# A two-layer decoder trunk on one core: how the first product's token blocks are evacuated, where the first RMSNorm's squares and token scale stand, and the last piece of the output

## The chip, the core and the metric

The kernel runs on one core of one Trainium2 chip. The metric is the device time of one execution in microseconds. The core's engines are TensorE (PE in the profile, its weight loads PEld), VectorE (DVE), ScalarE (ACT), GpSimd (POOL) and SyncE (SP, which here only issues transfers). An engine works its own queue in order; semaphores hold an instruction until what it needs is done.

## What is computed

A decoder of two layers over 256 tokens of width 2048 in float32: a layer of dilated window attention and a layer of latent attention, each with a SwiGLU block, and a last RMSNorm. The change works at the very start and at the very end. The start is this, cut from the reference:

```python
def rms_norm(x, g):
    y = x32 * lax.rsqrt(jnp.mean(x32 * x32, axis=-1, keepdims=True) + NORM_EPS)
    return (y * g.astype(jnp.float32)).astype(x.dtype)
...
xn = rms_norm(h, attn_norm_g[layer])
qkv = (xn @ w_qkv).reshape(b, s, N_A_GROUPS, 3, A_HEADS, A_HEAD_DIM)
...
return rms_norm(h, final_norm_g)
```

The token scale (the rsqrt) is one number per token, so the kernel multiplies x by the gain first, starts the products at once, and applies the scale to the results.

## The kernel before

Every matrix product runs in a split form: each operand is a rounded part (`hi`, or columns 0 to 255 of a block of `xT`) and a residue (`lo`, or columns 256 to 511), and three matmuls per block and token half (hi by hi, hi by lo, lo by hi) add up in PSUM. ScalarE makes the rounded parts by a copy, VectorE the residues by subtracting.

`first_product` is the first of the products for the values of four heads (a quad), with three products (g = 0, 1, 2) of 16 blocks each (k = 0 to 15, 128 columns of x each). It runs before any transposed x exists, so it makes it on the way, in eight steps q of two blocks. `turn(q)` lets TensorE transpose two blocks of both token halves into one PSUM bank (L673). `tokens(q, kk)` takes block 2q + kk out of that bank: `put_split` writes the rounded part by ScalarE (L421) and the residue by VectorE (L422), both times the gain. `weights(q, ...)` casts the weights of the step on ScalarE (L689) and makes their residue on VectorE (L690). `products(k)` issues six matmuls (L699). After the turn of step q come the products of block 2q - 1 and 2q; after the last turn blocks 13, 14 and 15. The order on ScalarE, VectorE and TensorE in this part is that of the code (`manual_schedule`); elsewhere a scheduler may reorder.

Weights come in units through `WeightStream`: three buffers of raw weights, each refilled by SP when the residue that last read it is done; units 0 and 1 serve step 0 and 1, unit 2 steps 2 and 3, unit 3 steps 4 and 5, unit 4 steps 6 and 7. Units 5 on are the second product's, four units to a product; `product` makes hi and lo of a unit two units ahead (L152, L153) and runs `x_stationary` (L522 to L524).

`norms(i)` squares and sums one of five column pieces of x: pieces 0 and 1 on VectorE (L431), 2 to 4 on ScalarE (L434), two instructions each. `token_stats` sums the pieces (L463, L457), takes the power -0.5 on GpSimd (L458) and splits the scale into a power of two and a remainder (L471, L473). Both are spread over all partitions by a matmul (`across`: L481, L484, L485) into `R2` and `R`. `to_v` evacuates a product to v with the scale as factor (L814); until then its accumulator is held, and there are two accumulators. `by_row` (L492) scales `xT` by `R2` in place in the third product. `Later` holds closures that are called so many ticks (units) on. L315 turns the other gain vectors.

At the end, `end1` finishes the last 512 columns of each token half: add, square, power on GpSimd (L1171), and scale the whole row in five pieces, stored in four (L1182).

Of the kernel before, what the change touches and what calls it, by code (L numbers as in the profile page):

```python
# [10 lines left out]
F32 = mybir.dt.float32  # L11
# [3 lines left out]
ALU = mybir.AluOpType  # L15
# [23 lines left out]
LAG_S, LAG_V = 2, 3  # L39
WARM = 8  # L40

# [206 lines left out]
def kernel(ctx, tc, consts, x, attn_norm_g, ffn_norm_g, a_w_qkv, a_w_o, kv_norm_g,  # L248
# [21 lines left out]
    def big_tile(shape, dtype, name):  # L270
        return big.tile(shape, dtype, tag="big", name=name)
# [389 lines left out]
    ssq_x = small.tile([P, NT, len(X_CHUNKS)], F32, name="ssq_x", tag="ssq_x", bufs=1)  # L661
    xT = big_tile([P, KD, 2 * S], F32R, "xT_a")
    def first_product():

# [4 lines left out]
        def turn(q):  # L669
            banks[q] = ps = bank()  # L670
            for kk in range(2):
                for t in range(NT):
                    nc.tensor.transpose(out=ps[:, kk * S + t * P:kk * S + (t + 1) * P],  # L673
                                        in_=xt[:, t, (2 * q + kk) * P:(2 * q + kk + 1) * P], identity=ident)

        def tokens(q, kk):
            k = 2 * q + kk
            put_split(xT[:, k, 0:S], xT[:, k, S:2 * S], banks[q][:, kk * S:(kk + 1) * S], g_attn0[:, k:k + 1])

# [21 lines left out]

        def norms(i):
            c0, w = X_CHUNKS[i]
            for t in range(NT):
                squares(xt[:, t, c0:c0 + w], ssq_x[:, t, i:i + 1], on_vector=i < 2)

        with tc.manual_schedule(engines=ORDERED | {mybir.EngineType.PE}):
            turn_attn()
            turn(0)
            weights(0, (0,), nc.vector.tensor_copy)  # L710
            tokens(0, 0)
            tokens(0, 1)
            weights(0, (1,))
            ws.load(4)
            products(0)
            for q in range(1, KD // 2):
                turn(q)
                for kk in range(2):
                    if q == 1:
                        weights(q, (kk,))  # L720
                    elif kk == 0:
                        weights(q, (0, 1))
                    tokens(q, kk)
                if q in (1, 3, 5):
                    later.tick()
                    ws.load(5 + q // 2)
                if q > 2:
                    norms(q - 3)
                products(2 * q - 1)
# [13 lines left out]
    def token_stats():  # L743

        rstd = token_scale(ssq_x, "rstd")
        r2_a, rem_a = parted(rstd)
        later.put(1, lambda: row_a.update(R2=across(r2_a, "R2", ap)))
        later.put(2, lambda: row_a.update(R=across(rem_a, "R")))
        for name, src, by in (("sc", rem_a, P ** -0.5), ("nsc", rem_a, -(P ** -0.5))):
            stats[name] = small.tile([P, NT], F32, name=name, tag=name, bufs=1)  # L750
            nc.vector.tensor_scalar(out=stats[name], in0=src, scalar1=by, scalar2=None, op0=ALU.mult)
        return rstd, rem_a

# [50 lines left out]
    for quad in range(HEADS // 4):  # L804
        vs = [ap.tile([P, NT, 512], F32, tag=f"v{g}", name=f"v{g}", bufs=1) for g in range(NG)]
        seven = SEVEN_V[quad]
        if quad == 0:
            acc0 = first_product()
            rstd, rem_a = token_stats()
        rv = rem_a if seven else rstd  # L810

        def to_v(v, src, rv=rv):
            for t in range(NT):
                nc.scalar.activation(out=v[:, t, :], in_=src[:, t, :], func=AF.Copy, scale=rv[:, t:t + 1])  # L814
# [343 lines left out]
    def end1(acc, t):  # L1158
# [12 lines left out]
        nc.gpsimd.tensor_tensor(out=r, in0=v, in1=mhalf[:, :1], op=ALU.pow)  # L1171
        nc.vector.tensor_tensor(out=h, in0=h, in1=fin["g"][:, 3 * 512:], op=ALU.mult)
        for a, b, on, queue in ((0, 512, 0, nc.sync), (512, 1024, 1, nc.scalar), (1024, 1536, 0, nc.sync),
                                (1536, 1792, 1, None), (1792, 2048, 0, nc.scalar)):
            piece = stream[0][:, t, a:b]
            if on:
                nc.scalar.activation(out=piece, in_=piece, func=AF.Copy, scale=r)
            else:
                nc.vector.tensor_scalar(out=piece, in0=piece, scalar1=r, scalar2=None, op0=ALU.mult)
            if queue:  # L1180
                a = min(a, 1536)
                queue.dma_start(out=ov[:, t, a:b], in_=stream[0][:, t, a:b])  # L1182

# [31 lines left out]
```

## Time and profile before

| quantity | value |
|---|---|
| median of 3 runs | 2652.59 us (2652.28 to 2652.73) |
| profiled execution | 2653.16 us, its span from first to last instruction 2651.4 us |
| TensorE clock granted | 0.999 |
| PE busy in the first 36.2 us from 4.5 us on | 30.14 of 31.70 us |
| ScalarE and VectorE busy there | 19.30 and 19.24 us |
| ScalarE's evacuations L421 waiting for VectorE's residue L422 | 8.3 us in 8 waits |
| VectorE's weight residues L690 waiting for the cast L689 | 6.2 us in 6 waits |
| DMA share from 8 to 24 us | 1.03 to 1.06 (full) |

Times in the trace are counted from the span's start. Idle time of an engine counts only where TensorE waits for it in the end, since TensorE's busy share of the whole span is 99%.

### The profile page before, as it was taken

What the parts mean: (1) busy time and instruction counts of PE and PEld (TensorE: products, weight loads), DVE (VectorE), ACT (ScalarE), POOL (GpSimd) and SP (SyncE); (2) the same over time, 40 slices, a digit from 0 to 9 for tenths busy, and PEclk for the clock granted to TensorE, in tenths of its full rate; (3) what the DMA queues carried; (4) which work ended last, traced back from release to release, by engine and by line L of the source; (5) the groups of instructions that cost most, each with busy time, mean ns of one, the idle gap of its engine ahead of it and who ended that gap; (6) DMA issues with size and microseconds to landing.
All of it is one profiled execution on the core that took longest, in us unless ns stands there. A gap on an engine that the chain in (4) does not pass through costs nothing.

```text
span 2651.4 us, 33136 instructions
## 1 busy us (share of the span) xinstructions
PE 2636.6 (99%) x12852; PEld 2211.9 (83%) x12852; DVE 2123.7 (80%) x2513; ACT 1324.5 (50%) x1406; POOL 106.9 (4%) x120
## 2 busy tenths in 40 slices
PE   9999999999999999999999999999999999999998
PEld 7888888888888888888888888888888888888887
DVE  5776777777677789987888887688789888898886
ACT  5444444444444455554554455565555545554554
POOL 0000000000000000001001100000000001001000
PEclk9999999999999999999999999999999999999999
DMA  7544655555555557678768867544466787768875
GB/s 252 191 161 163 203 173 172 178 184 164 174 178 170 196 175 222 206 222 255 218 214 231 245 200 231 167 155 135 154 209 208 219 238 229 221 205 248 237 225 164
DMA packets 324381, 529.39 MB, mean 200 GB/s; under 512 B 17960, under 2 KB 121088, under 8 KB 323840
## 3 DMA queue, kind: packets, MB, share of 16 engines
q1 hardware_dynamic: 305200, 492.33, 56.1%
q0 software_dynamic: 18112, 33.56, 8.2%
q8 instruction: 100, 1.64, 0.3%
q10 hardware_dynamic: 912, 1.39, 0.2%
q14 instruction: 57, 0.47, 0.1%
HBM read 514.63 MB, written 2.10 MB: 195 GB/s over the span
## 4 chain that ended last, share of the span: by engine, by line
PE 96%; DVE 1%; ACT 1%; DMA 1%; issue 1%; SPq 0%; POOL 0%; POOLq 0%; DVEq 0%; ACTq 0%
PE acc L609 17%; PE acc L610 17%; PE acc L611 17%; PE acc L503 15%; PE acc L506 8%; PE bank L610 4%; PE bank L609 4%; PE bank L611 4%; PE acc L523 3%; PE acc L524 3%; PE acc L522 3%; PE bank L779 1%; PE bank L443 1%; PE bank L794 1%; PE bank L573 1%
## 5 line engine op out<-in xcount | busy, mean ns | idle before, releaser
L152 ACT CAST hi<-raw 128x2048 fp32r<-128x2048 f32 (+3 forms) x612 | 874.7, 1454 | 755.8 <-PE acc L503 281.1
L153 DVE TENSOR_TENSOR lo<-raw,hi 128x2048 fp32r<-128x2048 f32 (+3 forms) x612 | 1046.6, 1721 | 254.8 <-ACT hi L152 235.8
L609 PE MATMUL acc<-hi,xT_f 128*128 128x512 f32 x996 | 390.0, 392 | 0.0
L610 PE MATMUL acc<-lo,xT_f 128*128 128x512 f32 x996 | 388.1, 390 | 0.0
L611 PE MATMUL acc<-hi,xT_f 128*128 128x512 f32 x996 | 388.1, 390 | 0.0
L503 PE MATMUL acc<-xT_a,hi 128*128 128x512 f32 x1536 | 379.0, 395 | 0.0
L503 PEld LDWEIGHTS acc<-xT_a,hi 128*128 128x128 f32 x1536 | 281.6, 188 | 53.8
L152 ACT CAST th<-sums 128x1536 fp32r<-128x1536 f32 x104 | 154.4, 1485 | 198.8 <-DVE sums L177 125.9
L609 PEld LDWEIGHTS acc<-hi,xT_f 128*128 128x128 f32 x996 | 187.0, 188 | 39.5 <-ACT gate L959 0.8
L611 PEld LDWEIGHTS acc<-hi,xT_f 128*128 128x128 f32 x996 | 187.0, 188 | 39.4
L610 PEld LDWEIGHTS acc<-lo,xT_f 128*128 128x128 f32 x996 | 187.1, 188 | 38.8
L153 DVE TENSOR_TENSOR tl<-sums,th 128x1536 fp32r<-128x1536 f32 x104 | 182.4, 1754 | 35.3 <-ACT th L152 35.3
L506 PEld LDWEIGHTS acc<-xT_a,lo 128*128 128x128 f32 x1536 | 196.9, 191 | 7.6
L506 PE MATMUL acc<-xT_a,lo 128*128 128x256 f32 x1536 | 199.2, 283 | 0.0
L609 PE MATMUL acc<-hi,hT 128*128 128x512 f32 x412 | 161.0, 391 | 0.0
L610 PE MATMUL acc<-lo,hT 128*128 128x512 f32 x412 | 160.5, 389 | 0.0
L611 PE MATMUL acc<-hi,hT 128*128 128x512 f32 x412 | 160.5, 389 | 0.0
L177 DVE TENSOR_TENSOR sums<-raw,sums 128x1024 f32<-128x1024 f32 x104 | 127.4, 1225 | 3.5
L176 DVE TENSOR_TENSOR sums<-raw 128x512 f32<-128x512 f32 x104 | 71.5, 687 | 58.7 <-DMA raw<-in_ffn_w_down_dram 22.2
L610 PEld LDWEIGHTS acc<-lo,hT 128*128 128x128 f32 x412 | 77.4, 188 | 16.2
L611 PEld LDWEIGHTS acc<-hi,hT 128*128 128x128 f32 x412 | 77.3, 188 | 16.3
L609 PEld LDWEIGHTS acc<-hi,hT 128*128 128x128 f32 x412 | 77.4, 188 | 16.1
(357 smaller groups left out, 4090.0 us busy)
## 6 DMA issues: line engine op xcount, KB each, us to landing
raw<-in_ffn_w_gu_dram SPq DMA_DIRECT2D x292, 512.0 KB, 4.8
raw<-in_a_w_qkv_dram SPq DMA_DIRECT2D x118, 1024.0 KB, 5.0
raw<-in_ffn_w_down_dram SPq DMA_DIRECT2D x124, 512.0 KB, 5.3
raw<-in_ffn_w_gu_dram SPq DMA_DIRECT2D x120, 256.0 KB, 3.9
raw<-in_a_w_qkv_dram SPq DMA_DIRECT2D x51, 512.0 KB, 4.8
raw<-in_a_w_o_dram SPq DMA_DIRECT2D x32, 512.0 KB, 4.6
raw<-in_b_w_o_dram SPq DMA_DIRECT2D x32, 512.0 KB, 4.7
raw<-in_ffn_w_gu_dram POOLq DMA_DIRECT2D x60, 256.0 KB, 4.6
```

The lines of the kernel that those rows point to most:

```text
L152: cast = lambda: nc.scalar.copy(out=hi, in_=src)
L153: rest = lambda: nc.vector.tensor_tensor(out=lo, in0=src, in1=hi.bitcast(F32), op=ALU.subtract)
L176: tt(out=w[:, 1], in0=v[:, 0], in1=v[:, 2], op=ALU.subtract)
L177: tt(out=w[:, 0::2], in0=v[:, 1::2], in1=w[:, 1].unsqueeze(1).broadcast_to([P, 2, 512]), op=ALU.subtract)
L503: mm(out=acc[:, i, :], lhsT=sl(hi, kk), rhs=xT[:, k0 + kk, :], start=first and kk == 0, stop=False)
L506: mm(out=acc[:, i, 0:S], lhsT=sl(lo, kk), rhs=xT[:, k0 + kk, 0:S], start=False, stop=last and kk == nk - 1)
L522: mm(out=acc[:, t, :ncol], lhsT=xh, rhs=rhs(hi, kk), start=st, stop=False)
L523: mm(out=acc[:, t, :ncol], lhsT=xh, rhs=rhs(lo, kk), start=False, stop=False)
L524: mm(out=acc[:, t, :ncol], lhsT=xl, rhs=rhs(hi, kk), start=False, stop=sp)
L609: mm(out=out, lhsT=xh, rhs=wh, start=st, stop=False)
L610: mm(out=out, lhsT=xh, rhs=wl, start=False, stop=False)
L611: mm(out=out, lhsT=xl, rhs=wh, start=False, stop=sp)
```

## The change

Five things are changed. In `first_product` both blocks of a pair are evacuated by ScalarE, one after the other, and VectorE's two residues follow (`tokens`, `tokens_lo`). The squares of pieces 2 to 4 leave the first product and come one, two and three ticks into the second. `token_stats`, the two spreads and the evacuation of the first product to v come after them; the second product's order on ScalarE and VectorE is now that of the code as well. Seven matmuls on ones instead of eight open the kernel. At the end the multiplication by the final gain is no instruction of its own but part of scaling the last piece, which VectorE now does whole.

```diff
-WARM = 8
+WARM = 7
...
-        def tokens(q, kk):
+        def tokens(q, lo=(0, 1)):
+            for kk in range(2):
+                k = 2 * q + kk
+                nc.scalar.activation(out=xT[:, k, 0:S], in_=banks[q][:, kk * S:(kk + 1) * S], func=AF.Copy,
+                                     scale=g_attn0[:, k:k + 1])
+            for kk in lo:
+                tokens_lo(q, kk)
+
+        def tokens_lo(q, kk):
             k = 2 * q + kk
-            put_split(xT[:, k, 0:S], xT[:, k, S:2 * S], banks[q][:, kk * S:(kk + 1) * S], g_attn0[:, k:k + 1])
+            nc.vector.scalar_tensor_tensor(out=xT[:, k, S:2 * S], in0=banks[q][:, kk * S:(kk + 1) * S],
+                                           scalar=g_attn0[:, k:k + 1], in1=xT[:, k, 0:S].bitcast(F32),
+                                           op0=ALU.mult, op1=ALU.subtract)
...
             turn(0)
+            tokens(0, ())
             weights(0, (0,), nc.vector.tensor_copy)
-            tokens(0, 0)
-            tokens(0, 1)
+            tokens_lo(0, 0)
             weights(0, (1,))
+            tokens_lo(0, 1)
...
-                for kk in range(2):
-                    if q == 1:
-                        weights(q, (kk,))
-                    elif kk == 0:
-                        weights(q, (0, 1))
-                    tokens(q, kk)
+                if q == 1:
+                    weights(q, (0,))
+                    tokens(q, (0,))
+                    weights(q, (1,))
+                    tokens_lo(q, 1)
+                else:
+                    weights(q, (0, 1))
+                    tokens(q)
...
-                if q > 2:
+                if q in (3, 4):
                     norms(q - 3)
...
-        later.put(1, lambda: row_a.update(R2=across(r2_a, "R2", ap)))
-        later.put(2, lambda: row_a.update(R=across(rem_a, "R")))
+        later.put(2, lambda: row_a.update(R2=across(r2_a, "R2", ap)))
+        later.put(3, lambda: row_a.update(R=across(stats["rem"], "R")))
...
             acc0 = first_product()
-            rstd, rem_a = token_stats()
+            for i in range(2, len(X_CHUNKS)):
+                later.put(i - 1, lambda i=i: norms(i))
+            later.put(3, token_stats)
+            later.put(3, lambda vs=vs, acc0=acc0, to_v=to_v: to_v(vs[0], acc0))
         for g in (2,) if seven else range(NG):
+            if quad == 0 and g == 0:
+                continue
...
-            to_v(vs[g], acc0 if quad == g == 0 else product(x_stationary, xT, KD))
+            with tc.manual_schedule(engines=ORDERED) if quad == 0 and g == 1 else nullcontext():
+                acc = product(x_stationary, xT, KD)
+            to_v(vs[g], acc)
...
-        nc.vector.tensor_tensor(out=h, in0=h, in1=fin["g"][:, 3 * 512:], op=ALU.mult)
-        for a, b, on, queue in ((0, 512, 0, nc.sync), (512, 1024, 1, nc.scalar), (1024, 1536, 0, nc.sync),
-                                (1536, 1792, 1, None), (1792, 2048, 0, nc.scalar)):
...
+        for i in range(4):
+            piece = chunk(t, i)
+            if i == 3:
+                nc.vector.scalar_tensor_tensor(out=piece, in0=piece, scalar=r, in1=fin["g"][:, 3 * 512:],
+                                               op0=ALU.mult, op1=ALU.mult)
+            elif i == 1:
                 nc.scalar.activation(out=piece, in_=piece, func=AF.Copy, scale=r)
             else:
                 nc.vector.tensor_scalar(out=piece, in0=piece, scalar1=r, scalar2=None, op0=ALU.mult)
-            if queue:
...
+            (nc.sync, nc.scalar)[i % 2].dma_start(out=ov[:, t, i * 512:(i + 1) * 512], in_=piece)
```

What stands on the queues before and after. In the names, `raw` is a weight buffer as loaded, `hi` and `lo` its two parts, `bank` a pair's transposed blocks, `junk` the squares' unused output; the numbers tell buffers of one name apart. ScalarE in steps 5 and 6 of the first product, before:

```order
L689 CAST hi_244<-raw_148 128x1024
L421 ACTIVATE xT_a_118<-bank_268,g_attn_97 128x256 [waits PE_49]
L421 ACTIVATE xT_a_118<-bank_268,g_attn_97 128x256 [waits DVE_49]
L434 ACTIVATE junk_287,ssq_x_117<-xt_99 128x512 [waits DMAHW7_49]
L434 ACTIVATE junk_289,ssq_x_117<-xt_99 128x512 [waits DMAHW2_49]
L689 CAST hi_308<-raw_171 128x1024 [waits DMAHW5_49,Activation_49]
L421 ACTIVATE xT_a_118<-bank_303,g_attn_97 128x256 [waits PE_49]
L421 ACTIVATE xT_a_118<-bank_303,g_attn_97 128x256 [waits DVE_49]
```

and after:

```order
L704 CAST hi_243<-raw_147 128x1024
L684 ACTIVATE xT_a_117<-bank_267,g_attn_96 128x256 [waits PE_49]
L684 ACTIVATE xT_a_117<-bank_267,g_attn_96 128x256
L704 CAST hi_303<-raw_170 128x1024 [waits DMAHW5_49,DVE_49]
L684 ACTIVATE xT_a_117<-bank_298,g_attn_96 128x256 [waits PE_49]
L684 ACTIVATE xT_a_117<-bank_298,g_attn_96 128x256
```

The second evacuation of a pair no longer waits for VectorE, and the squares between it and the next cast are gone. VectorE at the end of the first product, before:

```order
L690 TENSOR_TENSOR lo_309<-raw_171,hi_308 128x1024 [waits Activation_49]
L422 SCALAR_TENSOR_TENSOR xT_a_118<-bank_332,g_attn_97,xT_a_118 128x256 [waits Activation_49] x2
L463 TENSOR_REDUCE ssum_372<-ssq_x_117 128x2 [waits DVE_49,Activation_49]
L457 TENSOR_SCALAR rsq_v_375<-ssum_372 128x2 [waits DVE_49]
L471 TENSOR_SCALAR r2_378<-rstd_374 128x2 [waits Pool_49]
L473 TENSOR_SCALAR rem_379<-rstd_374 128x2
L481 TENSOR_SCALAR R2_433<-ident_93,r2_378 128x128 [waits DVE_49]
L751 TENSOR_SCALAR sc_382<-rem_379 128x2 [waits DVE_49]
L751 TENSOR_SCALAR nsc_384<-rem_379 128x2
L481 TENSOR_SCALAR R2_433<-ident_93,r2_378 128x128
L153 TENSOR_TENSOR lo_354<-raw_221,hi_353 128x1024 [waits DMAHW6_49,Activation_49]
```

and after:

```order
L705 TENSOR_TENSOR lo_304<-raw_170,hi_303 128x1024 [waits Activation_49]
L691 SCALAR_TENSOR_TENSOR xT_a_117<-bank_323,g_attn_96,xT_a_117 128x256 [waits PE_49,Activation_49]
L691 SCALAR_TENSOR_TENSOR xT_a_117<-bank_323,g_attn_96,xT_a_117 128x256
L153 TENSOR_TENSOR lo_341<-raw_220,hi_340 128x1024 [waits DMAHW6_49,Activation_49]
L153 TENSOR_TENSOR lo_341<-raw_220,hi_340 128x1024 [waits Activation_49]
```

The second product's first weight residue follows the token residues directly. The second residue of a pair has no wait of its own any more, so the first one's wait covers both evacuations. The same scale instructions now stand after the residue of unit 9, the third product's first. On TensorE the seam between the products was:

```order
L699 MATMUL acc_127<-hi_308,xT_a_118 128x512
L522 MATMUL acc_388<-hi_353,xT_a_118 128x512 [waits Activation_49]
L484 MATMUL bank_436<-R2_433,ones_82 128x256 [waits DVE_49,PE_49]
L315 MATMUL bank_471<-ident_93,g_row_280 128x56 [waits DMAHW2_49,DMAHW1_49,DMAHW3_49,DMAHW0_49,PE_49]
L523 MATMUL acc_388<-lo_354,xT_a_118 128x512 [waits DVE_49]
```

and is:

```order
L714 MATMUL acc_126<-hi_303,xT_a_117 128x512
L522 MATMUL acc_361<-hi_340,xT_a_117 128x512 [waits Activation_49]
L523 MATMUL acc_361<-lo_341,xT_a_117 128x512 [waits DVE_49]
L524 MATMUL acc_361<-hi_340,xT_a_117 128x512
L522 MATMUL acc_361<-hi_340,xT_a_117 128x512
```

The spread of R2 (L484) and L315 left the seam: L315 stands a product's half further on, the two spreads in the third product.

More of the change, by code (lines that the diff above doesn't have):

```diff
@@ L1 @@
 import math
-from contextlib import ExitStack
+from contextlib import ExitStack, nullcontext
 import numpy as np
@@ L662, with norms @@
     xT = big_tile([P, KD, 2 * S], F32R, "xT_a")
+    def norms(i):
+        c0, w = X_CHUNKS[i]
+        for t in range(NT):
+            squares(xt[:, t, c0:c0 + w], ssq_x[:, t, i:i + 1], on_vector=i < 2)
     def first_product():
@@ L700, in products @@
                    start=k == 0 and x == 0 and w is hi, stop=k == KD - 1 and x == S)
[L702 to L705, printed above, removed]
         with tc.manual_schedule(engines=ORDERED | {mybir.EngineType.PE}):
@@ L743, in token_stats @@
     def token_stats():
-        rstd = token_scale(ssq_x, "rstd")
-        r2_a, rem_a = parted(rstd)
-        later.put(1, lambda: row_a.update(R2=across(r2_a, "R2", ap)))
-        later.put(2, lambda: row_a.update(R=across(rem_a, "R")))
-        for name, src, by in (("sc", rem_a, P ** -0.5), ("nsc", rem_a, -(P ** -0.5))):
+        stats["r"] = token_scale(ssq_x, "rstd")
+        r2_a, stats["rem"] = parted(stats["r"])
+        later.put(2, lambda: row_a.update(R2=across(r2_a, "R2", ap)))
+        later.put(3, lambda: row_a.update(R=across(stats["rem"], "R")))
+        for name, by in (("sc", P ** -0.5), ("nsc", -(P ** -0.5))):
             stats[name] = small.tile([P, NT], F32, name=name, tag=name, bufs=1)
-            nc.vector.tensor_scalar(out=stats[name], in0=src, scalar1=by, scalar2=None, op0=ALU.mult)
-        return rstd, rem_a
+            nc.vector.tensor_scalar(out=stats[name], in0=stats["rem"], scalar1=by, scalar2=None, op0=ALU.mult)
     row_a = {}
@@ L806, with to_v @@
         seven = SEVEN_V[quad]
+        def to_v(v, src, kind="rem" if seven else "r"):
+            for t in range(NT):
+                nc.scalar.activation(out=v[:, t, :], in_=src[:, t, :], func=AF.Copy, scale=stats[kind][:, t:t + 1])
         if quad == 0:
             acc0 = first_product()
-            rstd, rem_a = token_stats()
[L810 to L814, printed above, removed]
+            for i in range(2, len(X_CHUNKS)):
+                later.put(i - 1, lambda i=i: norms(i))
+            later.put(3, token_stats)
+            later.put(3, lambda vs=vs, acc0=acc0, to_v=to_v: to_v(vs[0], acc0))
         for g in (2,) if seven else range(NG):
+            if quad == 0 and g == 0:
+                continue
             if quad == 0 and g == NG - 1:
@@ L1171, in end1 @@
         nc.gpsimd.tensor_tensor(out=r, in0=v, in1=mhalf[:, :1], op=ALU.pow)
-        nc.vector.tensor_tensor(out=h, in0=h, in1=fin["g"][:, 3 * 512:], op=ALU.mult)
-        for a, b, on, queue in ((0, 512, 0, nc.sync), (512, 1024, 1, nc.scalar), (1024, 1536, 0, nc.sync),
-                                (1536, 1792, 1, None), (1792, 2048, 0, nc.scalar)):
-            piece = stream[0][:, t, a:b]
-            if on:
+        for i in range(4):
[4 more added lines that the diff above has]
+            elif i == 1:
                 nc.scalar.activation(out=piece, in_=piece, func=AF.Copy, scale=r)
@@ L1179, in end1 @@
                 nc.vector.tensor_scalar(out=piece, in0=piece, scalar1=r, scalar2=None, op0=ALU.mult)
-            if queue:
-                a = min(a, 1536)
-                queue.dma_start(out=ov[:, t, a:b], in_=stream[0][:, t, a:b])
+            (nc.sync, nc.scalar)[i % 2].dma_start(out=ov[:, t, i * 512:(i + 1) * 512], in_=piece)
     ffn(xT, rstd, finish1, end1)
```

## The prediction

> **What bounds the kernel now.** I read the page's busy table first.
>
> ```profile
> PE 2636.6 (99%) x12852; PEld 2211.9 (83%) x12852; DVE 2123.7 (80%) x2513; ACT 1324.5 (50%) x1406; POOL 106.9 (4%) x120
> ```
>
> TensorE (PE) is busy 99% of the span and no other engine above 80% (PEld's weight loads run under it), so only what TensorE stops waiting for can shorten the run. The rows' busy times overlap (a 0.39 us matmul is followed by the next after 0.23), which hides small waits; I therefore go by the starts of TensorE's rows, in the first 40 us, where the change works. A timeline row gives start, duration, engine, line, tile, and in brackets the idle time before it and what ended it. I call the eight pairs of blocks q = 0 to 7; L673 turns a pair, then two products of six matmuls each (L699) follow, three after the last turn.
>
> ```profile
> 22.60 0.60 PE L673 MATMUL bank<-ident,xt 128*128 128x128 f32 x4
> 25.85 0.60 PE L673 MATMUL bank<-ident,xt 128*128 128x128 f32 x4
> 30.17 0.60 PE L673 MATMUL bank<-ident,xt 128*128 128x128 f32 x4
> 35.65 0.40 PE L699 MATMUL acc<-hi,xT_a 128*128 128x512 f32 x1
> 36.13 0.49 PE L522 MATMUL acc<-hi,xT_a 128*128 128x512 f32 x1
> 37.33 0.67 PE L484 MATMUL bank<-R,ones 128*128 128x256 f32 x2 [0.70 <-DVE R L481]
> 37.93 0.27 PE L315 MATMUL bank<-ident,g_row 56*128 56x56 f32 x1
> 38.37 0.50 PE L523 MATMUL acc<-lo,xT_a 128*128 128x512 f32 x1 [0.17 <-DVE lo L153]
> 48.95 0.39 PE L524 MATMUL acc<-hi,xT_a 128*128 128x512 f32 x1
> 49.18 0.59 PE L484 MATMUL bank<-R,ones 128*128 128x256 f32 x2
> 49.84 0.40 PE L523 MATMUL acc<-lo,xT_a 128*128 128x512 f32 x1
> ```
>
> One turn with its two products takes 3.25 us in q = 5 (22.60 to 25.85), where TensorE hardly waits. The same work takes 4.32 us in q = 6 (25.85 to 30.17): 1.07 lost. In q = 7 it has six matmuls more, 6 x 0.23 (48.95 to 49.18 is one matmul's pace) = 1.38, so 4.63 are due; it takes 30.17 to 35.65 + 0.23 = 5.71: 1.08 lost. Then comes the seam to the second product (L522 on): its second matmul (L523) could start 0.46 after 35.65, at 36.11, but starts at 38.37, 2.26 later. What stands between and is real work: the row spread L484 costs 0.43 where nothing waits (48.95 to 49.84 is 0.89, less two matmuls of 0.23), and the turn L315 is one transpose where L673 is four in 0.60, so I take 0.15 (bounds 0 and 38.37 - 37.93 = 0.44). So the seam loses 2.26 - 0.43 - 0.15 = 1.68.
>
> What causes the loss stands in the other engines' rows of q = 5 to 7:
>
> ```profile
> 23.15 1.22 DVE L690 TENSOR_TENSOR lo<-raw,hi 128x1024 fp32r<-128x1024 f32 x1
> 23.24 0.47 ACT L421 ACTIVATE xT_a<-bank,g_attn 128x256 fp32r<-128x256 f32 x1 [0.27 <-PE bank L673]
> 24.80 0.47 ACT L421 ACTIVATE xT_a<-bank,g_attn 128x256 fp32r<-128x256 f32 x1 [1.08 <-DVE xT_a L422]
> 25.17 0.62 ACT L434 ACTIVATE junk<-xt 128x512 f32<-128x512 f32 x1
> 26.40 1.03 ACT L689 CAST hi<-raw 128x1024 fp32r<-128x1024 f32 x1
> 27.33 0.47 ACT L421 ACTIVATE xT_a<-bank,g_attn 128x256 fp32r<-128x256 f32 x1
> 27.46 1.23 DVE L690 TENSOR_TENSOR lo<-raw,hi 128x1024 fp32r<-128x1024 f32 x1 [1.67 <-ACT hi L689]
> 28.61 0.48 DVE L422 SCALAR_TENSOR_TENSOR xT_a<-bank,g_attn,xT_a 128x256 fp32r<-128x256 f32 x1
> 29.12 0.47 ACT L421 ACTIVATE xT_a<-bank,g_attn 128x256 fp32r<-128x256 f32 x1 [1.31 <-DVE xT_a L422]
> 31.79 1.23 DVE L690 TENSOR_TENSOR lo<-raw,hi 128x1024 fp32r<-128x1024 f32 x1 [1.68 <-ACT hi L689]
> ```
>
> ScalarE (ACT) evacuates one block at 23.24, stands still 1.08 us until VectorE (DVE) has made that block's residue, evacuates the second at 24.80, squares two pieces of x (the first at 25.17) and only then casts the next weights (26.40). VectorE waits 1.67 us for that cast, so the weights' residue (27.46 to 28.69) and the token residue behind it (28.61 to 29.09) come late to TensorE. q = 7 repeats it (1.68 us before 31.79).
>
> Before 21.2 us another limit rules. The last two rows are the window from 16 to 20 us (busy times, then clock, DMA share, GB/s) and the one load issued between 11 and 13 us, that of q = 6 and 7, with 9.8 us to landing:
>
> ```profile
> 7.99 0.43 PEld L673 LDWEIGHTS bank<-ident,xt 128*128 128x128 f32 x4 [0.22 <-DMA xt<-in_x_dram]
> 9.28 0.62 ACT L689 CAST hi<-raw 128x512 fp32r<-128x512 f32 x1 [1.06 <-DMA raw<-in_a_w_qkv_dram]
> 11.98 1.05 ACT L689 CAST hi<-raw 128x1024 fp32r<-128x1024 f32 x1 [0.46 <-DMA raw<-in_a_w_qkv_dram]
> 18.82 1.05 ACT L689 CAST hi<-raw 128x1024 fp32r<-128x1024 f32 x1 [0.53 <-DMA raw<-in_a_w_qkv_dram]
> 19.90 1.23 DVE L690 TENSOR_TENSOR lo<-raw,hi 128x1024 fp32r<-128x1024 f32 x1 [0.41 <-ACT hi L689]
> 21.18 0.19 PEld L699 LDWEIGHTS acc<-lo,xT_a 128*128 128x128 f32 x1 [0.37 <-DVE lo L690]
> ...
> 16.00:20.00 4.00, 4.00 (x23) 3.34 (x22) 2.89 (x8) 2.26 (x5) 0.00 (x0) 1.00 1.05 388
> ...
> raw<-in_a_w_qkv_dram SPq DMA_DIRECT2D x1, 1024.0 KB, 9.8
> ```
>
> The casts of q = 1, 2 and 4 wait for their weights from DMA (1.06, 0.46, 0.53 us), the second turn for x, and the 16 DMA engines are full (share 1.05, 388 GB/s). From the load at 18.82 a fixed chain leads to TensorE: cast 1.05, residue 1.23, matmul at 21.18. The change does not load less, so TensorE is at 21.18 and at 22.60 where it was.
>
> **The change, part by part.** *Evacuations in pairs.* The 16 evacuations and 16 residues stay; ScalarE no longer waits between the two of a pair, and VectorE's first residue now comes behind both evacuations. By the rows an evacuation holds ScalarE for 0.37 us (24.80 to 25.17), so that is the first residue's added delay. *Squares.* Six of 0.62 us leave ScalarE's queue in q = 5 to 7 for the second product. I walk q = 5 on, with both. Turn 5 ends at 23.20, evacuations at 23.24 and 23.61 (to 24.08); the cast of q = 6 follows at 24.0 to 25.0 (its weights were issued by 13 at the latest and took 9.8, so they land by 22.8). VectorE, even if its weight residue stays at 23.15 to 24.37, makes the two token residues by 25.2 and the weight residue of q = 6 at 25.2 to 26.4 (before 28.69). Turn 6 stays at 25.85 to 26.45; evacuations to 27.33, residues 27.4 to 28.2. TensorE needs the weight residue at 27.9 and the first token residue (27.9) at 28.1: no wait. So turn 7 comes at 25.85 + 3.25 = 29.10 instead of 30.17. The cast of q = 7 runs 27.2 to 28.3, its residue 28.3 to 29.5 (before 33.02); turn 7 ends at 29.7, evacuations to 30.6, token residues 30.6 to 31.5, the first (31.1) asked for at 31.4. The first product ends at 29.10 + 4.63 = 33.73, not 35.88. Gain 1.07 + 1.08 = 2.15.
>
> At q = 0 and 1 the first residue is not behind a long weight residue, and the 0.37 may lie on the path. TensorE then runs into the waits for x (0.22 at 7.99) and for weights (0.46 at 11.98) all the same, which take it up; so I take 0 (bounds 0 and 2 x 0.37 = 0.74).
>
> [...]
>
> *The token scale* (L463 to L481, the pow on POOL) moves behind the squares, to about 49 us.
>
> ```profile
> 35.17 0.16 DVE L463 TENSOR_REDUCE ssum<-ssq_x 128x2 f32<-128x10 f32 x1 [0.73 <-ACT junk L434]
> 35.62 0.70 POOL L458 TENSOR_TENSOR rstd<-rsq_v,mhalf 128x2 f32<-128x2 f32 x1 [35.17 <-DVE rsq_v L457]
> 36.93 1.26 ACT L814 ACTIVATE v<-acc,rstd 128x512 f32<-128x512 f32 x2
> 49.38 2.00 ACT L152 CAST hi<-raw 128x1024 fp32r<-128x1024 f32 x2 [2.69 <-PE acc L524]
> 60.70 1.27 ACT L814 ACTIVATE v<-acc,rstd 128x512 f32<-128x512 f32 x2 [3.43 <-PE acc L524]
> ```
>
> At the seam TensorE waited 0.70 for R, which needs the scale, and 0.17 for the residue queued on VectorE behind the scale's instructions. Without both, the cast for the second product runs 30.5 to 31.5, its residue 31.5 to 32.7, ahead of 33.73: the 1.68 go. The two spreads and L315 keep their 0.43, 0.43 and 0.15 in TensorE's queue, further back. What is moved on ScalarE: 3 x 2 squares, about 1.24 per tick, in a queue that waited 2.69 us per unit for TensorE (before 49.38). The first product's accumulator is now held until v (L814) reads it: cast at 49.38 - 3.8 = 45.6, done 47.6, last squares 48.8, then from the sum L463 to v 1.76 us (35.17 to 36.93) and v's 1.26: freed at 51.8. The third product needs it when the second ends, 60.70 - 3.8 = 56.9. Cover 5.1 us; each microsecond past it costs one. VectorE stands still for POOL's 0.70 with the next unit's weight residue behind it, which TensorE wants a unit after 56.9. Its two copies of R and R2 now stand among the scalings L492; TensorE waits for none of these before, so 0. POOL has nothing else near, SP issues the same loads: its queue gets to the next loads and the constants sooner by up to a pair's wait (1.08), because the residue that frees a buffer is sooner; cost in the rivals.
>
> *Seven opening matmuls for eight* come to nothing: the second turn waits for x at 7.99 either way.
>
> *The tail.* The multiplication by the final gain goes into the last piece.
>
> ```profile
> 2644.68 0.68 DVE L1172 TENSOR_TENSOR h<-h,gfin 128x512 f32<-128x512 f32 x1
> 2644.84 0.94 POOL L1171 TENSOR_TENSOR rstd_f<-v_f,mhalf 128x1 f32<-128x1 f32 x1 [6.31 <-DVE v_f L1170]
> 2645.81 1.15 DVE L1179 TENSOR_SCALAR h<-h,rstd_f 128x512 f32<-128x512 f32 x3 [0.45 <-POOL rstd_f L1171]
> 2646.33 0.81 SPq L1182 DMA_DIRECT2D out_dram<-h  x2
> 2647.49 0.34 ACTq L1182 DMA_DIRECT2D out_dram<-h  x1
> ```
>
> VectorE's 0.68 ran beside POOL's pow, so nothing is saved by itself. VectorE's last piece grows from 256 to 512 columns with a second input: three in 1.15 become two in about 0.8 and one of 0.68 (L1172's price), end 2647.29; ScalarE's half piece goes, and the last store starts about 2647.3 against 2647.49: -0.2. POOL's pow took 0.94 beside VectorE and 0.70 without it (at 35.62): up to -0.24, and this moves all four stores. Bounds 0 and -0.44; the middle term, -0.24, since the first store (2646.33) opens a megabyte of stores that the last must queue behind. [...]
>
> **Sum.** 1.07 + 1.08 + 1.68 + 0.24 = 4.07 us less. Against the profiled execution, 2653.16, that is 2649.09; the median of the three runs, 2652.59, is 0.57 lower, so 2648.5 there. The bound of 0.2%, about what a measurement of this kernel tells from no change, is 5.3 us: this stays inside it, on the fast side.
>
> **The rivals.** *Later weights.* The loads behind those of q = 4 (the next unit, then the constants) start about 1.1 us sooner on full DMA engines. If they share with it half and half, q = 4 lands 0.55 late, and that passes 1:1 to 21.18 and the end: 2649.1; all of it, 2649.6. Against: the engines are full anyway, and if they take loads in turn nothing moves. *Earlier weights.* If q = 4's load counts from its issue, which is also sooner (the residue that frees its buffer no longer stands behind the second token residue of q = 0), the wait of 0.37 at 21.18 goes: 2648.1, and with the tail's other 0.2, 2647.9. The full DMA row speaks against it. Even this stays short of 5.3. *Serial reads.* If the 0.37 of the bank lies on TensorE's path in all eight pairs, 2.96 come back: 2651.4. Against: in my walk TensorE asks 0.2 us later than the first residue is done even with the 0.37. *Slower:* the late accumulator. If the squares slip two units (a unit is 24 matmuls of 0.23, 5.5 us), v ends at 62.8, 5.9 past 56.9, and the time is 2648.5 + 5.9 = 2654.4; it turns slower than before when v ends after 61.0. The 5.1 us of cover speak against it. *No effect:* if the waits are only renamed, 2652.6; the two losses at q = 6 and 7 sit on rows with a named releaser, so unlikely.
>
> **How the numbers follow.** Forecast 0.70 (2647.9 to 2649.0), later weights 0.12, earlier weights 0.07, serial reads 0.06, slower 0.03, no effect 0.02. The range leaves out the last two, half of serial reads, and what is past the bounds: low 2647.3 (earlier weights, less 0.6 for reading starts from rows that round at each pair), high 2650.3 (all of later weights and 0.7). Over 0.2% faster needs 1.2 us more than the sum: part of earlier weights with an unseen gain, 0.08. Over 0.2% slower needs the slip of three units: 0.02. Within: 0.90.
>
> **What would show it.** In the profile after: ScalarE's second evacuation 0.37 after the first, with no wait for VectorE; turns at 22.6, 25.85, 29.1; the second product's first matmul at about 33.7 with the second 0.23 behind it; v's first evacuation near 50.5 and no wait of TensorE at 56.8; POOL's last pow at 0.70. A cast at 18.82 that moves, or a TensorE wait between 40 and 60 us, would make the forecast wrong.

## The result, and the profile after

The changed kernel takes 2648.86 us (median of 22 runs, 2648.45 to 2650.27) against 2652.74 us before (22 runs, 2652.13 to 2653.37): 3.88 us less. The ratio is 0.9986, on the fast side and inside the 0.2% bound; the lower end of its 95% interval, 0.9979 to 0.9992, just passes that bound. Forecast was 2648.5, with a range of 2647.3 to 2650.3. The profiled execution took 2650.08 us (span 2648.3), 1.2 us more than the median; part of that shows in its opening.

TensorE's busy time, from the page of the changed kernel:

```profile
PE 2635.4 (100%) x12850; PEld 2214.0 (84%) x12850; DVE 2123.2 (80%) x2511; ACT 1323.3 (50%) x1404; POOL 106.0 (4%) x120
```

TensorE's rows in the timeline of the changed kernel, from the turn of q = 5 to the seam (L678 turns a pair, L714 multiplies, L522 opens the second product):

```profile
23.91 0.60 PE L678 MATMUL bank<-ident,xt 128*128 128x128 f32 x4
...
27.12 0.60 PE L678 MATMUL bank<-ident,xt 128*128 128x128 f32 x4
...
30.31 0.60 PE L678 MATMUL bank<-ident,xt 128*128 128x128 f32 x4
...
34.65 0.39 PE L714 MATMUL acc<-hi,xT_a 128*128 128x512 f32 x1
34.88 0.39 PE L522 MATMUL acc<-hi,xT_a 128*128 128x512 f32 x1
35.11 0.39 PE L523 MATMUL acc<-lo,xT_a 128*128 128x512 f32 x1
```

A turn with its two products now takes 3.21 and 3.19 us (forecast 3.25; 4.32 before in q = 6), the last one 4.57 up to L522 (forecast 4.63), and L523 follows L522 by 0.23 (before 2.24). The two losses that the prediction wanted to remove are gone. But the turns come at 23.91, 27.12 and 30.31 where 22.6, 25.85 and 29.1 were forecast: the first product ends 1.00 us sooner than before (34.65 against 35.65), not 2.15.

ScalarE's and VectorE's rows of the same stretch:

```profile
24.54 0.84 ACT L684 ACTIVATE xT_a<-bank,g_attn 128x256 fp32r<-128x256 f32 x2 [1.41 <-PE bank L678]
25.27 1.05 ACT L704 CAST hi<-raw 128x1024 fp32r<-128x1024 f32 x1
25.41 0.88 DVE L691 SCALAR_TENSOR_TENSOR xT_a<-bank,g_attn,xT_a 128x256 fp32r<-128x256 f32 x2 [0.49 <-ACT xT_a L684]
```

ScalarE waits for TensorE alone and makes both evacuations in one row (x2). VectorE's two residues start when these end, at 25.41, and no TensorE row waits for either engine here: the 0.37 us by which the first residue is later are covered, as walked.

Why all of it stands 1.3 us late is told by TensorE's first rows, ten microseconds earlier:

```profile
1.05 3.36 PE L278 MATMUL bank<-ones 128*128 128x128 f32 x14 [1.05 <-DVE mhalf L412]
4.89 0.28 PE L293 MATMUL bank<-ident,g_attn_row 32*128 32x32 f32 x1 [0.48 <-DMA g_attn_row<-in_attn_norm_g_dram]
...
7.80 1.05 PE L714 MATMUL acc<-lo,xT_a 128*128 128x512 f32 x2
8.66 1.05 PE L714 MATMUL acc<-hi,xT_a 128*128 128x512 f32 x2
...
13.13 0.40 PE L714 MATMUL acc<-lo,xT_a 128*128 128x512 f32 x1
13.36 0.62 PE L714 MATMUL acc<-hi,xT_a 128*128 128x512 f32 x2
```

Two matmuls start every 0.86 us (7.80 to 8.66), 0.43 each; at 13.13 the next starts 0.23 later. TensorE ran at half pace until about 12.8 us in this execution. The window from 6 to 12.6 us (stretch and its length, TensorE's busy time and matmuls, granted clock, DMA share, GB/s), of the changed kernel:

```profile
6.00:12.60 6.60, 6.04 (x18) 1.00 1.03 370
```

and of the kernel before:

```profile
6.00:12.60 6.60, 5.95 (x27) 1.00 1.02 365
```

18 matmuls stand against 27, and the clock column reads 1.00 in both. It does not show the halving because the trace keeps the granted clock as records with a start and a length: the first record, at full clock, starts at 12.85 us in this profile and at 5.69 in that of before, and the column counts what lies before a first record as full. So here the spacing of the rows is the thing to read. In front of L293 stands a gap of 0.48 us, a wait for a DMA after the seven opening matmuls (two records each); before, with eight, there was none. Whether that gap was the cause became the first question.

ScalarE's evacuations to v, the late ones that could have held an accumulator:

```profile
50.49 1.27 ACT L822 ACTIVATE v<-acc,rstd 128x512 f32<-128x512 f32 x2 [1.29 <-POOL rstd L458]
57.27 1.27 ACT L822 ACTIVATE v<-acc,rstd 128x512 f32<-128x512 f32 x2 [3.44 <-PE acc L524]
```

The first accumulator is read out by 50.49 + 1.27 = 51.76 and the second product ends 5.5 us after that, just before 57.27. TensorE has no wait there.

The two pieces of work that the prediction moved back in TensorE's queue, L315 in the second product and a spread in the third:

```profile
45.53 0.39 PE L524 MATMUL acc<-hi,xT_a 128*128 128x512 f32 x1
45.85 0.27 PE L315 MATMUL bank<-ident,g_row 56*128 56x56 f32 x1
46.05 0.50 PE L522 MATMUL acc<-hi,xT_a 128*128 128x512 f32 x1
46.39 0.39 PE L523 MATMUL acc<-lo,xT_a 128*128 128x512 f32 x1
...
62.28 0.39 PE L524 MATMUL acc<-hi,xT_a 128*128 128x512 f32 x1
62.51 0.59 PE L484 MATMUL bank<-R,ones 128*128 128x256 f32 x2
63.17 0.40 PE L523 MATMUL acc<-lo,xT_a 128*128 128x512 f32 x1
```

From L524 at 45.53 to L523 at 46.39 are 0.86 us; two matmuls are 0.46 of them, so L315 costs 0.40, not 0.15. The spread costs 0.89 - 0.46 = 0.43, as taken.

The tail of the changed kernel, and the last matmul of the kernel before:

```profile
2640.09 0.39 PE L524 MATMUL acc<-hi,hT 128*128 128x512 f32 x1
2642.14 0.55 POOL L1189 TENSOR_TENSOR rstd_f<-v_f,mhalf 128x1 f32<-128x1 f32 x1 [6.68 <-DVE v_f L1188]
2643.24 0.81 SPq L1199 DMA_DIRECT2D out_dram<-h  x2
```

```profile
2642.79 0.39 PE L524 MATMUL acc<-hi,hT 128*128 128x512 f32 x1
```

GpSimd's power takes 0.55 (before 0.94), and from the last matmul's start to the first store pass 3.15 us (before 2646.33 - 2642.79 = 3.54): 0.39 less.

### The profile page after: what moved, and what is told of

Same layout as the page of the kernel before. It is cut to its first block, busy times and chain, and to the rows that moved or that the text cites. A ratio compares the mean times of both kernels' runs of the same rounds, so it can differ in the third digit from the quotient of the medians.

```text
span 2648.3 us, 33131 instructions
## 1 busy us (share of the span) xinstructions
PE 2635.4 (100%) x12850; PEld 2214.0 (84%) x12850; DVE 2123.2 (80%) x2511; ACT 1323.3 (50%) x1404; POOL 106.0 (4%) x120
## 4 chain that ended last, share of the span: by engine, by line
PE 97%; DVE 1%; ACT 1%; issue 1%; DMA 1%; POOL 0%; POOLq 0%; ACTq 0%; DVEq 0%
PE acc L609 17%; PE acc L610 17%; PE acc L611 17%; PE acc L503 15%; PE acc L506 8%; PE bank L610 4%; PE bank L609 4%; PE bank L611 4%; PE acc L522 3%; PE acc L524 3%; PE acc L523 3%; PE bank L791 1%; PE bank L443 1%; PE acc L714 1%; PE bank L806 1%
## 5 line engine op out<-in xcount | busy, mean ns | idle before, releaser
L153 DVE TENSOR_TENSOR lo<-raw,hi 128x2048 fp32r<-128x2048 f32 (+3 forms) x612 | 1046.5, 1721 | 255.0 <-ACT hi L152 236.5
L153 DVE TENSOR_TENSOR tl<-sums,th 128x1536 fp32r<-128x1536 f32 x104 | 182.3, 1753 | 35.8 <-ACT th L152 35.7
L176 DVE TENSOR_TENSOR sums<-raw 128x512 f32<-128x512 f32 x104 | 71.5, 687 | 57.8 <-DMA raw<-in_ffn_w_gu_dram 22.8
```

The lines of the kernel that those rows point to most:

```text
L153: rest = lambda: nc.vector.tensor_tensor(out=lo, in0=src, in1=hi.bitcast(F32), op=ALU.subtract)
L176: tt(out=w[:, 1], in0=v[:, 0], in1=v[:, 2], op=ALU.subtract)
```

## The experiments

All eight were timed in five rounds beside the kernel before, which took 2652.75 us. A profile is one execution of eleven; where it and the median tell different things, both are given.

### Only the pairs, only the squares and scale

x_pairs is the kernel before with the new `tokens` and its order in the loop:

```diff
-                for kk in range(2):
-                    if q == 1:
-                        weights(q, (kk,))
...
+                else:
+                    weights(q, (0, 1))
+                    tokens(q)
```

> The kernel before with the paired evacuations alone (squares, token scale, opening matmuls and tail as before). Theory A, the two main parts do the same work twice: with the waits between evacuations gone, ScalarE has room for the squares, so the turn of q = 7 comes at about 29.1 us (before 30.17), the first product ends near 33.7 (before 35.9), and the scale is ready early enough that the seam loses nothing beyond its two added matmul groups: 3.4 to 3.7 us less than before. Theory B, the parts add up: the pairs give only their half, 1.5 to 2.2 us less, with the seam's wait for R still 0.7. Theory C, the shared bank costs the pair order 0.37 us per pair on TensorE's path: less than 1 us gained.

x_squares is the kernel before with the other main part, the squares, `token_stats` and the evacuation to v moved into the second product, whose order on ScalarE and VectorE is fixed as in the changed kernel (no run separates that from the move):

```diff
-                if q > 2:
+                if q in (3, 4):
                     norms(q - 3)
...
+            for i in range(2, len(X_CHUNKS)):
+                later.put(i - 1, lambda i=i: norms(i))
+            later.put(3, token_stats)
+            later.put(3, lambda vs=vs, acc0=acc0, to_v=to_v: to_v(vs[0], acc0))
```

> The kernel before with the squares and the token scale moved into the second product, evacuations in the old order, opening matmuls and tail as before. Theory A: alone it also takes nearly all, 3.2 to 3.7 us less, since the cast for q = 7 no longer stands behind the squares and the seam is free of the scale. Theory B: 1.7 to 2.2 us less (the seam only). If the held accumulator or the later scale cost something, TensorE shows a wait between 40 and 65 us; I expect none.

x_pairs took 2650.08 us (2.67 less; ratio 0.9990, 0.9981 to 0.9999). x_squares took 2648.98 us (3.77 less; ratio 0.9986, 0.9977 to 0.9995), just past theory A's 3.2 to 3.7. x_pairs met no forecast by its time: 2.67 lies between theory A's 3.4 to 3.7 and theory B's 1.5 to 2.2. Its trace has theory A's early first product, but a seam that still stalls. The two parts overlap: their gains would add to 6.4, and together they give 3.9. The squares and scale alone give what the whole change gives, and they beat the pairs: 2648.47 to 2649.73 against 2649.59 to 2650.93, eleven runs each on one chip. TensorE at the seam, first of x_pairs, then of x_squares:

```profile
33.06 0.39 PE L522 MATMUL acc<-hi,xT_a 128*128 128x512 f32 x1
33.37 0.67 PE L484 MATMUL bank<-R,ones 128*128 128x256 f32 x2
34.41 0.50 PE L523 MATMUL acc<-lo,xT_a 128*128 128x512 f32 x1 [0.37 <-DVE lo L153]
```

```profile
33.26 0.39 PE L522 MATMUL acc<-hi,xT_a 128*128 128x512 f32 x1
33.49 0.40 PE L523 MATMUL acc<-lo,xT_a 128*128 128x512 f32 x1
```

Either part brings the second product forward from 36.13 to about 33.1 or 33.3. Only the moved scale clears the seam: 0.23 us from L522 to L523 against 1.35, of which 0.37 is a wait for the residue L153 behind the scale's instructions. ScalarE's waits in the first 36 us of x_squares, total first, then times and the longest:

```profile
ACT xT_a L421 <- DVE xT_a L422: 7.9, 8, 1.3
```

So the wait of ScalarE for VectorE's residue, which the prediction named first among the causes (8.3 us in eight waits before), is all but whole, 7.9 us, and costs nothing once the squares are gone. What binds is ScalarE's lap. From the rows of before, one lap at q = 6 goes from the evacuation at 24.80 to its like at 29.12 and takes 4.32 us: evacuation 0.37, squares 25.17 to 26.40, that is 1.23, cast 26.40 to 27.33, that is 0.93, and the other evacuation with the wait behind it 1.79. TensorE's turn takes 3.2. Without the squares the lap is 4.32 - 1.23 = 3.09, and x_squares's rows have just that, 24.45 to 27.54; without the wait it is 4.32 - 1.31 = 3.01, and x_pairs's, 22.71 to 25.93, is 3.22 with 0.22 of waiting for TensorE in it. Each cure is enough to come under 3.2, and what goes below that gains nothing, since TensorE's lap binds then. That is why the two parts do the same work twice.

### Only the scale

x_scale moves the token scale, the spreads and v, but leaves the squares in the first product:

```diff
             acc0 = first_product()
-            rstd, rem_a = token_stats()
+            later.put(1, token_stats)
+            later.put(1, lambda vs=vs, acc0=acc0, to_v=to_v: to_v(vs[0], acc0))
```

> The kernel before with the token scale, its two spreads and the evacuation to v moved one tick into the second product, while the squares of pieces 2 to 4 stay in the first product; old order of evacuations, old tail, eight opening matmuls. Theory A (the prediction's two terms are separate): q = 6 and 7 keep their losses of 1.07 and 1.08 us, the first product ends near 35.9 as before, and only the seam goes: 1.2 to 1.4 us less, 2651.4. Theory B (the squares hold ScalarE, and so the second product's first cast and residue, and the seam stalls for that instead): 0 to 0.7 us less, 2652.0 to 2652.7, with a wait of TensorE for lo (L153) at L523. Theory C (the scale's instructions alone were the brake): 2649.0, as with the squares moved too.

It took 2653.01 us (2652.17 to 2655.26; ratio 1.0001, 0.9992 to 1.0010). The median shows no gain; the interval, 2.1 us less to 2.7 more, doesn't exclude theory A's 1.4 by itself, so the trace has to decide. TensorE's rows at its seam, and ScalarE's before it:

```profile
35.17 0.39 PE L704 MATMUL acc<-hi,xT_a 128*128 128x512 f32 x1
35.68 0.49 PE L522 MATMUL acc<-hi,xT_a 128*128 128x512 f32 x1
36.94 0.50 PE L523 MATMUL acc<-lo,xT_a 128*128 128x512 f32 x1 [0.77 <-DVE lo L153]
```

```profile
33.98 0.62 ACT L434 ACTIVATE junk<-xt 128x512 f32<-128x512 f32 x1
34.59 5.78 ACT L152 CAST hi<-raw 128x1024 fp32r<-128x1024 f32 x6
```

The spread R and the scale are out of the seam, and TensorE still waits 0.77 us, now for the residue L153 alone. ScalarE squares until 34.59 and only then casts the second product's weights (a row of six casts), whose residue comes at 35.66 to TensorE at 36.94. This is theory B: with the squares in front, the seam's stall changes its releaser. Its gain at the seam, 2.24 to 1.26 us between L522 and L523, is little more than the 0.83 us of the spread and L315, which only went elsewhere (L315 to 31.65, into a wait of TensorE in the first product). Theory C falls with it. The profile is of the fastest of the eleven executions, 1.0 us below that of before in span, and its first product ends 0.48 us sooner (35.17 against 35.65). The lap is not what differs: ScalarE's second evacuations stand at 24.35, 28.67 and 32.99, 4.32 apart as before. Only the start does, 24.35 instead of 24.80, since the cast of q = 4 had no wait for its weights in this execution (18.30 against 18.82). So the prediction's seam term hangs on the squares too, not on the scale alone.

### The tail alone

x_tail has the new last pieces and nothing else:

```diff
-        nc.vector.tensor_tensor(out=h, in0=h, in1=fin["g"][:, 3 * 512:], op=ALU.mult)
...
+            if i == 3:
+                nc.vector.scalar_tensor_tensor(out=piece, in0=piece, scalar=r, in1=fin["g"][:, 3 * 512:],
+                                               op0=ALU.mult, op1=ALU.mult)
```

> The kernel before with the new tail alone. If POOL's pow was held up by VectorE's multiplication beside it, the pow takes 0.55 instead of 0.94 us and the end comes 0.4 us sooner behind TensorE's last matmul; if only the last store's issue counts, 0.2 us; if the stores' bandwidth alone counts, 0. In the timed runs 0.4 us is at the edge of what can be seen.

It took 2652.64 us (ratio 0.9999, 0.9990 to 1.0008), 0.11 less than before: not to be told from nothing. On its trace the stretch from the last matmul's start to the span's end is 8.18 us (before 8.61, changed kernel 8.21). GpSimd's last power in x_tail:

```profile
2645.07 0.55 POOL L1171 TENSOR_TENSOR rstd_f<-v_f,mhalf 128x1 f32<-128x1 f32 x1 [6.67 <-DVE v_f L1170]
```

The step is there in the trace, 0.40 to 0.43 us in two kernels, and too small for the timing.

### The opening: seven or eight matmuls, and the half pace

x_warm8 is the changed kernel with one line put back:

```diff
-WARM = 7
+WARM = 8
```

> The changed kernel with eight opening matmuls again. Theory A, the half pace of TensorE up to 12.6 us in the changed kernel's profile (matmuls 0.43 us apart) comes from the gap that the missing eighth matmul opens: the pace is 0.23 from the first product's start as in the kernel before, the first product ends at about 33.7 instead of 34.9, and the profiled span is 1.1 us shorter than the changed kernel's 2648.3; the timed median 0 to 0.5 lower. Theory B, the pace at the start varies from run to run whatever the number of matmuls: the eighth matmul changes nothing that stands out from the spread of the runs. Theory C, the late first product is the pair order's bank delay: it still ends at 34.9.

It took 2649.02 us (ratio 0.9985, 0.9976 to 0.9994). Its profile has the full pace and the second product's first matmul at 33.82, against 33.7 forecast; but the median is not below the changed kernel's, and the span, 2647.7, is 0.6 us shorter than in the changed kernel's profile where 1.1 was forecast. That speaks for a pace that changes from run to run. Two more runs ask directly. x_again is the changed kernel once more:

> The changed kernel once more, for its opening. Theory A (the half pace of TensorE, 0.43 us between matmuls up to 12.6 us, comes from the gap of 0.48 us that the missing eighth opening matmul leaves before L293): the gap and the half pace recur, the turns start near 9.5 and 14.3, the first product ends near 34.9. Theory B (the pace is a matter of chance and the gap is too): full pace 0.23 from about 8 us on, turns near 8.0 and 12.2, first product ends at 33.6 to 33.8, as with eight opening matmuls. Both: time 2648.9, within 0.4.

2648.77 us (2648.19 to 2649.64; ratio 0.9985, 0.9976 to 0.9994), and theory B's opening. TensorE's opening and its first product's end:

```profile
4.50 0.28 PE L293 MATMUL bank<-ident,g_attn_row 32*128 32x32 f32 x1
...
7.43 0.62 PE L714 MATMUL acc<-hi,xT_a 128*128 128x512 f32 x2
7.89 0.60 PE L678 MATMUL bank<-ident,xt 128*128 128x128 f32 x4
...
22.38 0.60 PE L678 MATMUL bank<-ident,xt 128*128 128x128 f32 x4
...
33.34 0.39 PE L522 MATMUL acc<-hi,xT_a 128*128 128x512 f32 x1
```

The same program had next to no gap before L293 (0.08 us), the full pace (two matmuls in 0.46, 7.43 to 7.89), and L522 at 33.34, 1.54 sooner than in its first profile. Its time, 2649.64, was only 0.44 below the first one's. Most of the lead was lost in one place far behind: by TensorE's rows x_again was 1.2 us ahead until 2395 us and 0.4 from 2418 us on. VectorE's row that combines two weight blocks there, in the first profile and then in x_again, and TensorE's next wait in x_again:

```profile
2391.50 0.69 DVE L176 TENSOR_TENSOR sums<-raw 128x512 f32<-128x512 f32 x1 [3.87 <-DMA raw<-in_ffn_w_down_dram]
```

```profile
2391.46 0.69 DVE L176 TENSOR_TENSOR sums<-raw 128x512 f32<-128x512 f32 x1 [5.06 <-DMA raw<-in_ffn_w_down_dram]
...
2395.74 0.19 PEld L610 LDWEIGHTS bank<-lo,hT 128*128 128x128 f32 x1 [0.55 <-DVE lo L153]
```

VectorE waits for a load of weights and starts at the same time in both, although x_again had come 1.2 us sooner; TensorE then waits for the residue made behind it, and at 2408.86 another 0.50 us for h (L997). The first profile has neither wait. Why the load landed no sooner was not traced; it shows how far single executions can be trusted here. x_before7 is the kernel before with `WARM = 7`, nothing else:

> The kernel before with seven opening matmuls and nothing else changed. Theory A (the missing matmul opens the gap): half pace up to about 12 us, turns of q = 1 and 2 at about 9.5 and 14.3 instead of 8.0 and 12.1. The time is 1 us longer only where the lateness outlasts the weights' limit at 18.8 us, so 0 to +1.1 us: 2652.7 to 2653.8. Theory B (chance): the opening of the profile of before, turns 8.0 and 12.1, 2652.7 within 0.3. Theory C (fewer opening matmuls let everything start 0.2 us sooner): 2652.5.

2652.71 us (ratio 0.9999, 0.9990 to 1.0008), 0.04 from before, which by time alone fits theories A and B. In its opening and in that of x_best (below, with eight opening matmuls) TensorE's rows read:

```profile
4.52 0.21 PE L293 MATMUL bank<-ident,g_attn_row 32*128 32x32 f32 x1 [0.26 <-DMA g_attn_row<-in_attn_norm_g_dram]
...
7.82 1.05 PE L699 MATMUL acc<-hi,xT_a 128*128 128x512 f32 x2
8.67 1.05 PE L673 MATMUL bank<-ident,xt 128*128 128x128 f32 x4
```

```profile
4.77 0.31 PE L293 MATMUL bank<-ident,g_attn_row 32*128 32x32 f32 x1
...
7.71 1.05 PE L704 MATMUL acc<-lo,xT_a 128*128 128x512 f32 x2
8.57 1.05 PE L704 MATMUL acc<-hi,xT_a 128*128 128x512 f32 x2
```

x_best has eight matmuls and no gap, and half pace all the same, until about 10.5 us; x_before7 has a gap of 0.26 and half pace until 10.8. x_scale, with eight, had it until 10.2. So the missing matmul is not the cause that theory A made it: in ten profiles half pace beyond 7 us came four times, twice with seven matmuls and twice with eight, with and without a gap, and the medians do not follow the number of opening matmuls (seven against eight: 2652.71 and 2652.75 us for the kernel before, 2648.77 and 2649.02 for the changed one).

The clock's records say more. x_before7 is the one profile whose clock column shows the halving, in the same window from 6 to 12.6 us:

```profile
6.00:12.60 6.60, 6.17 (x21) 0.74 1.02 364
```

Its records are full clock from 3.98 to 7.39 us, half to 10.80, then full: steps of 3.41 us. In the stretch that ended with the fall to half TensorE had stood idle 1.36 us (0.26 and 1.10, the wait before 6.43). In the nine other profiles the first record at full clock comes at the end of 3.41 us in which TensorE's rows have next to no gap (0.08 us at most); in six it starts at 4.5 to 5.7 us, in x_scale at 10.24, in x_best at 10.48 and in the changed kernel's first profile at 12.85. Only x_before7 has records of the steps; in the others they are counted back from the first record in the same 3.41 us, which is an estimate. In these last three the step so counted just before, which brought no full clock, holds the wait of 0.56 us for the first evacuation (in x_best 6.13 to 6.69 us). In the changed kernel's first profile the step before that, 2.61 to 6.02, holds the gap of 0.48 as its only idle time, so there the gap may well have counted too. By this count the steps fall differently in the program from profile to profile (the same program's first full record stands at 12.85 us in one and at 5.72 in the other), so whether they catch one of these waits is a matter of the single execution. That idle time in a step holds the clock back is read from these ten profiles and not tested by a run, and how much it takes is not shown: x_before7's clock rose at 3.98 with 0.49 us of idle time in the step before.

Of these two profiles of one program, TensorE works from 1.05 and 1.06 us on, long before either record. In the first the gap of 0.48 and the wait of 0.56 come ahead of 12.85; in the second, x_again, the gap is 0.08 and the wait of 0.56, at 5.83 to 6.39, comes after 5.72.

### The change without its pairs

x_best is x_squares with the new tail: old order of evacuations, eight opening matmuls.

```diff
-            tokens(0, ())
             weights(0, (0,), nc.vector.tensor_copy)
-            tokens_lo(0, 0)
+            tokens(0, 0)
+            tokens(0, 1)
```

> The moved squares and scale with the new tail, but the old order of evacuations and eight opening matmuls: the change without its pairs. Theory A (the pairs add nothing once the squares are gone; the tail gives its 0.4 us): 2648.6, at or below the changed kernel (2648.9 here). Theory B (the pairs still carry the first product): 2649.3 or more, with waits of TensorE at q = 6 and 7 and the first product's end past 34.0. Theory C (no tail gain that can be timed): 2649.0, as the moved squares and scale alone.

2648.74 us (2648.40 to 2649.69; ratio 0.9984, 0.9976 to 0.9993), beside 2648.77 for the changed kernel on the same chip. It lies between theory A's 2648.6 and theory C's 2649.0, which eleven runs don't tell apart, and below theory B's 2649.3. Without the pairs the time is the same. No kernel of these beats the changed one by more than can be measured. Even with half pace in its opening it reached L522 at 33.70: the half pace ended at 10.5, and of the 1.26 us that its turn of q = 2 was behind x_again's (13.12 against 11.86) 0.35 were left at q = 5 (22.73 against 22.38). The weights' limit around 18 us took up the rest: x_again's cast of q = 4 waited 1.56 us there for its load. In the changed kernel's first profile it ended at 12.8, too late for that.

## Why the prediction was right, and where its steps were not

*The first product: 2.15.* Right as a mechanism and in size, 3.21 and 3.19 us for a turn and 4.57 for the end; x_again gives L522 at 33.34 and x_warm8 at 33.82 around the forecast 33.73. In the changed kernel's own profile only 1.00 showed, because of the half pace. The step that failed there is "TensorE is at 21.18 and at 22.60 where it was": the weights' limit is a floor, and TensorE may come to it late. Its turn of q = 5 was at 23.91. In x_again, where it was not late, the floor showed, with ScalarE's cast of q = 4 waiting for its weights, 0.23 us sooner than before:

```profile
18.59 1.05 ACT L704 CAST hi<-raw 128x1024 fp32r<-128x1024 f32 x1 [1.56 <-DMA raw<-in_a_w_qkv_dram]
```

*What caused it.* The prediction named ScalarE's wait for VectorE's residue and the squares together, and walked them together. x_squares shows the wait to be free once the squares are gone, x_pairs the squares to be free in the first product once the wait is gone. The named releaser with the largest total (8.3 us) was no cause by itself; the lap's sum was. The size of 2.15 holds either way, because both cures end at TensorE's own lap.

*The seam: 1.68.* The stall went wholly (L523 0.23 behind L522), but the step that sized L315 failed: taken as 0.15 between bounds of 0 and 0.44, it measures 0.40. By that the term is 2.26 - 0.43 - 0.40 = 1.43. And "without both", R and the scale, was not enough: x_scale took both away and TensorE waited 0.77 for the residue.

*The tail: 0.24.* 0.39 to the first store, 0.40 to the end of the span. The power was priced at 0.70 by a row of two columns; this one has one column and takes 0.55 with VectorE out of its way. Beside VectorE's multiplication the power took 0.94, so it is held back by 0.39 us: before, it began 0.16 us after the start of VectorE's 0.68 and ended 0.42 behind its end, a little less than the 0.55 that it would take there if it had stood still until then. What holds it back was not shown. VectorE is not held back: its 0.68 is what a row of the same shape with two inputs takes where GpSimd has no row beside it (0.69 at 2391.50, L176).

*Sum.* With the terms as measured, 2.15 + 1.43 + 0.40 = 3.98; the timing gave 3.88 and, again, 3.98. The mechanism was right, but that the forecast of 4.07 came so near was in part luck: the term of the seam was 0.25 too large and that of the tail 0.16 too small. In the single profile the account is 1.00 + 1.43 for the first product and the seam against 2.70 at the last matmul. The 0.27 between them is no single gain: row by row the lead over the profile of before is about 2.6 us at 400 us, 2.2 at 600, 2.4 at 1400 and 2.7 from 2000 us on, and what moved it was not traced.

*Costs taken as nothing.* Seven opening matmuls: 0.04 us in x_before7, nothing; but the reason given, that the second turn waits for x at 7.99 either way, did not hold, since x_again turned at 7.89 without a wait for x. The first residue's 0.37 at q = 0 and 1: x_best and x_again, without and with it, differ by 0.03. The late accumulator: 5.5 us of cover where 5.1 were forecast (its 51.8 came true in the first profile only because TensorE was late as a whole; in x_again v begins at 48.95). Serial reads, later weights and earlier weights: the first is excluded as a tax of 2.96 by x_best against x_again (2648.74 and 2648.77), and by turns of 3.2 us with the pairs in place; that the shared bank itself costs the 0.37 was not shown, the first residue stands behind both evacuations in any case. The other two, of 0.4 to 1.1 us, stay open. The sign that the prediction set for them, a cast at 18.82 that moves, can't tell: where that cast waited for its weights it came at 18.53 to 19.30 in three profiles with neither main part changed, and at 18.30 to 19.05 in five with one or both.

## What to carry to other kernels

For an engine that serves another in laps, add up its lap (work and waits, from one row to its like) and compare it with the lap of the engine it serves; what brings it under that is gain, and everything beyond is nothing, so two cures for one lap do not add. A stall's releaser names who was last, not who was late: take that one away and the next in the queue takes its place, as the casts behind the squares did. Gains of some 0.1% are to be read from the relative steps in a trace, since one execution's opening can shift all the marks after it, and a load far behind can take a lead back.

## What was not expected of the hardware

TensorE ran at half pace, 0.43 us between matmuls of 512 columns instead of 0.23, until 10.2 to 12.85 us in four of ten profiled executions. In three of them the clock column reads 1.00 there, because the trace has no clock record yet; in x_before7 it reads 0.74 over 6 to 12.6 us. It cost up to 1.5 us at the seam (34.88 against 33.34 for the same program). In nine of the ten profiles the full clock began at the end of 3.41 us in which TensorE stood idle 0.08 us at most. GpSimd's power on one column took 0.94 us beside a VectorE multiplication of two inputs and 0.55 without it.
